# A two-layer attention and SwiGLU trunk on one core: where the bias tables are sent, and where the squares and 1/rms of the second norm stand

## The chip, the core and the metric

The kernel runs on one core of one Trainium2 chip. The metric is the device time of one execution in microseconds (us), the median of several. The engines are TensorE (PE, matmuls), VectorE (DVE), ScalarE (ACT), GpSimd (POOL) and SyncE (SP, whose queue issues nearly all DMAs). All data are float32.

## The reference, cut to what matters

Sequence and width are 1024, there are two layers. Each layer does the following, and a last RMSNorm closes the trunk.

```python
h = rms_norm(x, g_attn[l]) * (1 + sc1) + sh1          # modulated by c @ w_mod
q.., k.., v.. = split(h @ w_in[l])                    # 4 + 6 + 6 heads, three groups
# A: 2-D neighbourhood attention, bias from rpb_na[l]
# B: windowed attention, T5 bias by distance, sink logits
# C: dense attention, q/k normed, rotary
x = x + gate1 * (rms_norm_per_group(concat(A, B, C)) @ w_o[l])
h = rms_norm(x, g_ffn[l]) * (1 + sc2) + sh2
u, g = split(h @ w_gu[l]); x = x + gate2 * ((silu(u) * g) @ w_down[l])
```

## The kernel before

**Products.** Every float32 operand of a product is split into a high part and the rest (`whi`/`wlo` for weights; names that end in h and l for activations), and `mm3` (lines 205 to 208) makes three matmuls of a product. ACT makes the high part, DVE or POOL the difference (`split_tile`, 156 to 168). A weight column comes by SP into `wst`, of which there are two buffers.

**Stages.** The start turns x, makes the modulation by a matrix-vector product over `w_mod` (tiles `gm`) and does the first columns of group C. The order of PE, ACT, DVE and SP is written out there: `pin` makes an `Engine` keep the order of the text. Where no `pin` is on, a scheduler sets the order on each engine and may draw an instruction ahead of where the text has it. Then come the projections of layer 0 (A, B and C columns, then v, whose weights `wst` and `wsv` SP loads), the stream of the attention's 64 pairs, the o-projection with its residuals, gate/up, down. Layer 1 repeats this from the projections on.

**Tables.** Group A's bias comes from a skewed table in DRAM, one for each layer: three DMAs spread `rpb_na` over it, one of 930 KB and two of 248 elements by 16 by 8. Lines 828 to 837 send both tables at the end of the start. Group B's bias rows are made by `bias_rows` (1024 to 1031) in layer 0's projections: a product, a subtraction on DVE, one store to `rowB` and six broadcasts of it into `skB`, which the attention reads as `bz`. The pieces of a table overlap, so that one waits for the landing of the one before.

**The o-projection.** Its loop takes eight output columns in the order 6, 7, 0 to 5 (1847 to 1865). `residual` adds each column's product to x (tile `xb`) on DVE for the second half of the tokens. The first half is done before it: `square_sum` (400 to 411) squares its eight blocks on ACT and adds them on DVE to `ssq`; `rstd_rows` then runs in two steps, `rstd_cols` (four matmuls into `ps_st`, a root on ACT, a reciprocal on DVE) and `spread` (four transposes into `ps_r`, from which DVE reads 1/rms as a row). After the loop `square_sum` is called for the second half.

**Gate/up.** A product of 1024 by 1024 blocks is made from seven (`PRODUCTS`, 221 to 224), each of four k groups with three matmuls. For the first `EARLY = 7` column blocks q the products "11" and "21", which need the first half of the tokens alone, are made first, from the weight columns that `first_cols` loads and splits. Beside them the second half is normed: `rstd_cols` for it stands after the products of q = 0, `spread` after the first product of q = 1, and `t2_part`, `t3_part` and `t4_part` make the parts t1 to t4 and "22" of the activations (tiles `ht1h` to `ht4l`, `h22h`, `h22l`). Then the main loop makes the other products of q = 0: t2, t1, t3, "22", t4. The products "12" to "22" are combined in `gu_product`, whose copies from PSUM are `u` and `sg`; POOL multiplies `sg` by `u`, and the tile that a finished copy goes to can be one whose x block has to be read first, so that the copy ahead of "22" waits for the last part of t4.

Of the kernel before, what the change touches and what calls it, by code (L numbers as in the profile page):

```python
# [10 lines left out]
F32 = mybir.dt.float32  # L11
F32R = mybir.dt.float32r
I32 = mybir.dt.int32
AF = mybir.ActivationFunctionType
ALU = mybir.AluOpType
# [4 lines left out]
P = 128  # L20
D = 1024
S = 1024
KC = D // P
H = 512
FF = 2816
# [57 lines left out]
def bc(ap, shape):  # L83
    return ap.to_broadcast(shape)
# [3 lines left out]
def trunk(ctx: ExitStack, tc, A, C, out):  # L88
# [5 lines left out]
    def pin(engines, on):  # L94
        for e in engines:
            e.pinned = on

    def open_pool(name, bufs=1, side="left", space=None):
        kw = dict(name=name, bufs=bufs, side=side, reuse_waits="tile")
        if space is not None:  # L100
            kw["space"] = space
            if space == PSUM:
                kw.pop("side")
        cm = tc.tile_pool(**kw)
        p = cm.__enter__()
        return cm, p
# [63 lines left out]
    def split_w(src, a=1, hl=None, eng=None):  # L170


        st = stage()
        for dst, s in src(parts(st, a)):
            sp.dma_start(dst, s)
        return split_tile(st, a, hl, eng)
# [101 lines left out]
            self.fill()  # L278
            return self.have.pop(0)

    def product(num, banks, bank, a, b, m):
        if num in (1, 2, 5):
            banks[bank] = psl.tile([P, 512], F32, name="ps_w", tag="mm")
        ps = banks[bank]
        for k in range(m):
            mm3(
                ps, a[0][:, k], a[1][:, k], b[0][:, k], b[1][:, k],
                num in (1, 2, 5) and k == 0, k == m - 1, skip_group_check=True,
            )
        return ps  # L290


# [104 lines left out]
            yield  # L397


    def square_sum(ntp, xt, half, bufs=2):  # L400
        ssq = ntp.tile([P, H], F32, name="ssq", tag="ssq", bufs=bufs)
        c = slice(half * H, (half + 1) * H)
        for n in range(KC):
            if n == 0:
                act.activation(ssq, xt[:, n, c], AF.Square)
                continue
            sq = ntp.tile([P, H], F32, name="sq", tag="sq", bufs=2)
            act.activation(sq, xt[:, n, c], AF.Square)
            dve.tensor_tensor(out=ssq, in0=ssq, in1=sq, op=ALU.add)
        return ssq  # L410

    def rstd_cols(ssqs, width, nt, sp_, psp, tag="mm", newton=False):

# [330 lines left out]
    ps = spread(rxs[0], 0, psl)  # L744
# [80 lines left out]
    for n in (4, 6):  # L825
        h_blocks(1, rows, (n, n + 1))
    sp.dma_start(sinkc, bc(A["sink_sw"].rearrange("l h -> (l h)")[None, :], [P, 12]))
    for l in range(2):
        rpb = A["rpb_na"][l].rearrange("h i d -> (h i d)")
        for o, n in ((OVER, 1860), (0, OVER), (OVER + 1860, OVER)):  # L830
            sp.dma_start(
                bass.AP(
                    tensor=skA[l].tensor, offset=skA[l].offset + o,
                    ap=[[8 * LA + 31, 16], [LA + 1, 8], [1, n]],
                ),
                bc(rpb[None, None, 0:n], [16, 8, n]),
            )
    pin((pe, act, dve, sp), False)
    close(s2_cm)
    dve.tensor_scalar(out=sinkc, in0=sinkc, scalar1=-1.0, scalar2=None, op0=ALU.mult)  # L840
# [3 lines left out]
    for l in range(2):  # L844
# [14 lines left out]
        def qk_tile():  # L859
            return qkp.tile([P, 5, S], F32R, name="qk", tag="qk", bufs=2)  # L860
# [161 lines left out]
        def bias_rows():  # L1022


            ps = psl.tile([P, 512], F32, name="ps_b", tag="mm")
            for i in range(2):
                pe.matmul(ps[0:6], t5h[:, i, :], oneh, start=(i == 0), stop=(i == 1))
            dve.tensor_tensor(out=mB, in0=mB, in1=ps[0:6], op=ALU.subtract)
            sp.dma_start(rowB, mB)
            for h in range(6):  # L1030
                sp.dma_start(skB[h], bc(rowB[h][None, :], [P, 512]))

# [619 lines left out]
        for n in range(-AHEAD - 1, N + 1):  # L1654
# [19 lines left out]
                what()  # L1674
            if n == 50:
                yq = qk_tile()
            if n == 8:
                edges_make()
            if n == 54:
# [67 lines left out]
        def residual(ps, n, c, g0):  # L1747
            dve.scalar_tensor_tensor(
                out=xt[:, n, c], in0=ps, scalar=mod[:, g0 + n : g0 + n + 1], in1=xt[:, n, c],
                op0=ALU.mult, op1=ALU.add,  # L1750
            )
# [88 lines left out]
        def h_shift_split(b, i, src, sh):  # L1840
            hi, lo = (t[:, i] for t in hb[b])
            act.activation(hi, src, AF.Identity, bias=sh)
            shifted_sub(lo, src, sh, f32(hi))

        mp_cm, mp = open_pool("mp", side="left")
        ssq = square_sum(ntp, xt, 0, 1)
        for i, n in enumerate((6, 7, 0, 1, 2, 3, 4, 5)):
            w = wc[i] if i < KC - NK else w_next()
            if i < 4:
                spill(0, range(2 * i, 2 * i + 2))  # L1850
            ps = psl.tile([P, 512], F32, name="ps_o", tag="mm")
            o_cols(
                ps, w, range(8), lambda ki: y1[0][:, korder[ki], :],
                lambda ki: y1[1][:, korder[ki], :],
            )
            residual(ps, n, slice(H, S), 16)
            if i == 1:
                norm = rstd_rows(ssq, ntp, psl)
                next(norm)
            if i == 3:  # L1860
                rows = next(norm)
                for k in range(KC):
                    h_norm(k, 0, rows)
                    h_shift_split(("11", "21")[k % 2], k // 2, xt[:, k, 0:H], shift(k))
        ssq = square_sum(ntp, xt, 1, 1)
        spill(1)
        close(mp_cm)
        close(y1_cm)
# [41 lines left out]

        sg, quads = {}, {}

        def gu_product(q, p, a):
            num, b, bank = p
            up = q % 2
            t = quads.setdefault(q, {})
            ps = product(num, t, bank, a, hb[b], 4)
            e, o = sg.get(q // 2, (None, None))
            lo, hi = slice(0, H), slice(H, S)

# [74 lines left out]
            sg[b] = [x_tile(4 + 2 * (b % 2) + i, [P, S], "sg") for i in range(2)]  # L1995


        def first_cols(c0):
            rows = w_gu[:, c0 : c0 + P].rearrange("(k h p) n -> h p k n", h=2, p=P)
            return split_w(  # L2000
                lambda v: [(v[:, 4 * i : 4 * i + 4], rows[i]) for i in range(2)], KC, eng=dve
            )

        dsh = ffp.tile([P, 4], F32, name="dsh")
        for i in range(4):
            sub(dsh[:, i : i + 1], shift(2 * i + 1), shift(2 * i))
        EARLY = 7
        early = [first_cols(q % 2 * FF + q // 2 * 2 * P) for q in range(4)]
        raw0 = None
        spare = cp.tile([P, 1024], F32, name="spare", tag="acc")  # L2010

# [27 lines left out]

        mods_due = mod_stream(psl, (ntp, "sq", 2, H), (l + 1, 1 - l))  # L2040
        bs = []
        rows = None
        norm = rstd_rows(ssq, ntp, psl)
        ahead = Ahead(gu_parts())
        for q in range(EARLY):
            for i in range(2):
                a = [w[:, 4 * i : 4 * i + 4] for w in early[q]]
                gu_product(q, PRODUCTS[i], a)
                if (q, i) == (1, 0):
                    rows = next(norm)  # L2050
            if q + 4 < EARLY:
                early.append(first_cols((q + 4) % 2 * FF + (q + 4) // 2 * 2 * P))
            elif raw0 is None:
                raw0 = gu_raw(0)
            if q == 0:
                next(norm)
            if 1 <= q < 5:
                bs.append(t2_part(q - 1, rows))
            if q == 1:
                t3_part(0, *bs[0])  # L2060
                t4_part(0, *bs[0])
            if q == EARLY - 2:
                ahead.fill(5)
# [360 lines left out]
```

## Time and profile before

| | us |
|---|---|
| median of 3 runs | 2408.71 |
| range of the runs | 2406.3 to 2409.22 |
| the profiled execution | 2405.48 |
| its span | 2403.5 |
| PE busy in it | 2354.1 |
| DVE busy | 1783.6 |
| ACT busy | 1203.9 |
| POOL busy | 760.7 |

The page of the profile gives busy times by engine, the span in slices, and the costliest groups. A row of the timeline gives the start, the busy time, the engine, the line, the operation with its tiles (out <- in) and shape, how many of them stand in the row, and in square brackets how long the engine was idle before it and what ended that. All instructions of the engines carry L51, the line of the helper that issues them, so that they are told apart by their tiles. SPq is SP's queue of DMA issues. A row of the windows gives the busy time of engines in a stretch, with the clock that PE was granted (1.00 is full speed), the busy share of the DMA engines and the GB/s. A row of the waits gives what an engine waited for: us in total, times, and the longest.

### The profile page before, as it was taken

The numbers are of one execution on the slowest core, as the hardware profiler recorded it, in microseconds if no ns is written. First come the engines' busy times: TensorE is split into PE (matmuls) and PEld (weight loads), VectorE is DVE, ScalarE is ACT, GpSimd is POOL, SyncE is SP. The second block draws the span as 40 slices with busy tenths as digits, with TensorE's granted clock in tenths as the row PEclk, the third lists the DMA queues.
The fourth block names the chain that finished last, engine by engine and source line by source line (L and its number), as shares of the span: only waits on it lengthen the run. The fifth ranks groups of instructions, "written<-read, shape, count | busy, mean of one in ns | idle before, by whom it ended". The sixth has DMA issues, their size and how long they took to land. (4 is left out here: it accounts for less than half of the span.)

```text
span 2403.5 us, 34024 instructions
## 1 busy us (share of the span) xinstructions
PE 2354.1 (98%) x11953; PEld 1966.3 (82%) x11953; DVE 1783.6 (74%) x2826; ACT 1203.9 (50%) x2296; POOL 760.7 (32%) x767
## 2 busy tenths in 40 slices
PE   8999999999999999999999999999999999999998
PEld 5788898788788888888888889987878888888786
DVE  6757898977957776497866689988787675537765
ACT  5322888944543433344533158897454334334443
POOL 1522445610344444200145224464005443430001
PEclk9999999999999999999999999999999999999999
DMA  8667206064345343687434841332634443329643
GB/s 292 170 184 241 73 12 183 18 210 129 105 142 166 127 149 101 194 255 248 150 108 126 256 122 27 81 113 74 212 103 132 145 146 106 117 91 295 210 127 109
DMA packets 300497, 351.40 MB, mean 146 GB/s; under 512 B 51620, under 2 KB 221948, under 8 KB 300328
## 3 DMA queue, kind: packets, MB, share of 16 engines
q1 hardware_dynamic: 277368, 332.85, 44.2%
q10 hardware_dynamic: 21504, 12.59, 2.0%
q0 software_dynamic: 1456, 3.81, 0.4%
q8 instruction: 94, 1.54, 0.3%
q14 instruction: 75, 0.61, 0.1%
HBM read 267.38 MB, written 85.79 MB: 147 GB/s over the span
## 5 line engine op out<-in xcount | busy, mean ns | idle before, releaser
L51 PE MATMUL ps_d<-wpt 128*128 128x512 f32 x1848 | 425.8, 391 | 3.3 <-ACT wpt L51 1.5
L51 PEld LDWEIGHTS ps_d<-wpt 128*128 128x128 f32 x1848 | 345.3, 188 | 78.7 <-DVE wpt L51 2.9
L51 POOL TENSOR_SCALAR pr<-pr,rs 128x384 f32<-128x384 f32 (+2 forms) x252 | 191.9, 775 | 282.4 <-DVE rs L51 260.1
L51 POOL TENSOR_TENSOR sg<-sg,u 128x512 f32<-128x512 f32 x86 | 124.4, 1448 | 352.1 <-ACT sg L51 227.9
L51 PE MATMUL pv<-pt,vs 128*128 128x256 f32 x1088 | 180.9, 296 | 7.2 <-DVE y L51 3.3
L51 DVE TENSOR_TENSOR pt<-T,pt 128x512 fp32r<-128x512 f32 x272 | 178.1, 681 | 9.4 <-ACT pt L51 7.8
L51 ACT COPY u<-ps_w 128x512 f32<-128x512 f32 x128 | 75.2, 587 | 209.3 <-PE ps_w L51 209.3
L51 PE MATMUL T<-identr,pr 128*128 128x128 f32 x1176 | 173.3, 273 | 1.0 <-ACT rb L51 0.6
L51 ACT CAST pt<-T 128x512 fp32r<-128x512 f32 x272 | 152.7, 586 | 39.7 <-PE T L51 37.4
L51 POOL TENSOR_TENSOR wpt<-ws,wpt 128x512 fp32r<-128x512 f32 x80 | 112.4, 1406 | 179.2 <-ACT wpt L51 137.9
L51 ACT CAST wpt<-w 128x512 fp32r<-128x512 f32 x154 | 95.5, 620 | 137.2 <-PE ps_d L51 129.2
L51 PEld LDWEIGHTS pv<-pt,vs 128*128 128x128 f32 x1088 | 144.6, 189 | 22.1 <-DVE y L51 11.7
L51 DVE TENSOR_TENSOR wpt<-w,wpt 128x512 fp32r<-128x512 f32 x154 | 111.0, 720 | 64.7 <-ACT wpt L51 64.3
L51 PEld LDWEIGHTS T<-identr,pr 128*128 128x128 f32 x1176 | 138.7, 140 | 17.3 <-ACT rb L51 1.0
L51 DVE SCALAR_TENSOR_TENSOR acc<-wmt,condT,acc 128x512 f32<-128x512 f32 (+1 forms) x98 | 104.7, 1078 | 63.8 <-DMA wmt<-in_w_mod_dram 63.4
L51 ACT CAST wpt<-ws 128x512 fp32r<-128x512 f32 x176 | 107.8, 622 | 63.4 <-PE ps_w L51 26.8
L51 ACT CAST wpt<-graw 128x512 fp32r<-128x512 f32 x154 | 95.0, 617 | 72.7 <-DMA graw<-gpd 61.0
L51 DVE TENSOR_TENSOR wpt<-ws,wpt 128x512 fp32r<-128x512 f32 x96 | 87.0, 915 | 54.0 <-ACT wpt L51 53.9
L51 DVE TENSOR_REDUCE rs<-sC 128x1 f32<-128x1024 f32 x96 | 116.5, 1218 | 12.2 <-PE sC L51 10.8
L51 DVE TENSOR_TENSOR wlo<-wst,whi 128x1024 fp32r<-128x1024 f32 x68 | 85.6, 1260 | 49.5 <-ACT whi L51 45.5
L51 ACT CAST whi<-wst 128x1024 fp32r<-128x1024 f32 x70 | 73.2, 1049 | 93.0 <-PE ps_o L51 46.6
L51 DVE TENSOR_TENSOR wpt<-graw,wpt 128x512 fp32r<-128x512 f32 x154 | 110.3, 716 | 10.9 <-ACT wpt L51 10.9
(301 smaller groups left out, 6103.1 us busy)
## 6 DMA issues: line engine op xcount, KB each, us to landing
wr<-in_w_gu_dram SPq DMA_DIRECT2D x92, 512.0 KB, 4.3
gpd<-sg SPq DMA_DIRECT2D x154, 256.0 KB, 4.5
graw<-gpd SPq DMA_DIRECT2D x76, 512.0 KB, 3.7
w<-in_w_down_dram SPq DMA_DIRECT2D x110, 256.0 KB, 5.4
wmt<-in_w_mod_dram SPq DMA_DIRECT2D x48, 512.0 KB, 5.8
qk<-qkd SPq DMA_DIRECT2D x44, 512.0 KB, 7.1
wst<-in_w_o_dram SPq DMA_DIRECT2D x32, 512.0 KB, 4.2
wmt<-in_w_mod_dram SPq DMA_DIRECT2D x64, 256.0 KB, 4.5
```

What stands on the lines that cost most here:

```text
L51: ins = op(*args, **kwargs)
```

## The change

Four edits go together.

- The table of layer 1 and the six broadcasts into `skB` are issued in the text of layer 0's attention (n is the pair): `skB` at n = 1, 3 and 5, the table at n = 7. Layer 0's table stays where it was.
- `square_sum` becomes a generator that takes the blocks in the residuals' order 6, 7, 0 to 5. The second half's squares start after the residual at i = 4 and go on with one block for each residual.
- The first weight columns of gate/up are loaded within the o loop: column 0 at i = 4, FF and 2P at i = 6, FF + 2P behind it. ACT and DVE keep the written order from the residual at i = 5 until the end of q = 0.
- 1/rms stands inside the second product of q = 0: `rstd_cols` after its k = 0, `spread` after k = 2. `product` and `gu_product` take a table of calls for that.

```diff
@@ -278,7 +278,7 @@
             self.fill()
             return self.have.pop(0)
 
-    def product(num, banks, bank, a, b, m):
+    def product(num, banks, bank, a, b, m, inside=()):
         if num in (1, 2, 5):
             banks[bank] = psl.tile([P, 512], F32, name="ps_w", tag="mm")
         ps = banks[bank]
@@ -287,6 +287,8 @@
                 ps, a[0][:, k], a[1][:, k], b[0][:, k], b[1][:, k],
                 num in (1, 2, 5) and k == 0, k == m - 1, skip_group_check=True,
             )
+            if k in inside:
+                inside[k]()
         return ps
 
 
@@ -397,17 +399,17 @@
             yield
 
 
-    def square_sum(ntp, xt, half, bufs=2):
-        ssq = ntp.tile([P, H], F32, name="ssq", tag="ssq", bufs=bufs)
+    def square_sum(ntp, xt, half, order):
+        ssq = ntp.tile([P, H], F32, name="ssq", tag="ssq", bufs=1)
         c = slice(half * H, (half + 1) * H)
-        for n in range(KC):
-            if n == 0:
+        for n in order:
+            if n == order[0]:
                 act.activation(ssq, xt[:, n, c], AF.Square)
-                continue
-            sq = ntp.tile([P, H], F32, name="sq", tag="sq", bufs=2)
-            act.activation(sq, xt[:, n, c], AF.Square)
-            dve.tensor_tensor(out=ssq, in0=ssq, in1=sq, op=ALU.add)
-        return ssq
+            else:
+                sq = ntp.tile([P, H], F32, name="sq", tag="sq", bufs=2)
+                act.activation(sq, xt[:, n, c], AF.Square)
+                dve.tensor_tensor(out=ssq, in0=ssq, in1=sq, op=ALU.add)
+            yield ssq
 
     def rstd_cols(ssqs, width, nt, sp_, psp, tag="mm", newton=False):
 
@@ -825,7 +827,7 @@
     for n in (4, 6):
         h_blocks(1, rows, (n, n + 1))
     sp.dma_start(sinkc, bc(A["sink_sw"].rearrange("l h -> (l h)")[None, :], [P, 12]))
-    for l in range(2):
+    def table(l):
         rpb = A["rpb_na"][l].rearrange("h i d -> (h i d)")
         for o, n in ((OVER, 1860), (0, OVER), (OVER + 1860, OVER)):
             sp.dma_start(
@@ -835,6 +837,8 @@
                 ),
                 bc(rpb[None, None, 0:n], [16, 8, n]),
             )
+
+    table(0)
     pin((pe, act, dve, sp), False)
     close(s2_cm)
     dve.tensor_scalar(out=sinkc, in0=sinkc, scalar1=-1.0, scalar2=None, op0=ALU.mult)
@@ -1027,8 +1031,6 @@
                 pe.matmul(ps[0:6], t5h[:, i, :], oneh, start=(i == 0), stop=(i == 1))
             dve.tensor_tensor(out=mB, in0=mB, in1=ps[0:6], op=ALU.subtract)
             sp.dma_start(rowB, mB)
-            for h in range(6):
-                sp.dma_start(skB[h], bc(rowB[h][None, :], [P, 512]))
 
 
 
@@ -1674,6 +1676,11 @@
                 what()
             if n == 50:
                 yq = qk_tile()
+            if l == 0 and n in (1, 3, 5):
+                for h in (n - 1, n):
+                    sp.dma_start(skB[h], bc(rowB[h][None, :], [P, 512]))
+            if l == 0 and n == 7:
+                table(1)
             if n == 8:
                 edges_make()
             if n == 54:
@@ -1842,9 +1849,16 @@
             act.activation(hi, src, AF.Identity, bias=sh)
             shifted_sub(lo, src, sh, f32(hi))
 
+        def first_cols(c0):
+            rows = w_gu[:, c0 : c0 + P].rearrange("(k h p) n -> h p k n", h=2, p=P)
+            return split_w(
+                lambda v: [(v[:, 4 * i : 4 * i + 4], rows[i]) for i in range(2)], KC, eng=dve
+            )
+
         mp_cm, mp = open_pool("mp", side="left")
-        ssq = square_sum(ntp, xt, 0, 1)
-        for i, n in enumerate((6, 7, 0, 1, 2, 3, 4, 5)):
+        *_, ssq = square_sum(ntp, xt, 0, order)
+        order = (6, 7, 0, 1, 2, 3, 4, 5)
+        for i, n in enumerate(order):
             w = wc[i] if i < KC - NK else w_next()
             if i < 4:
                 spill(0, range(2 * i, 2 * i + 2))
@@ -1853,7 +1867,20 @@
                 ps, w, range(8), lambda ki: y1[0][:, korder[ki], :],
                 lambda ki: y1[1][:, korder[ki], :],
             )
+            if i == 5:
+                pin((act, dve), True)
             residual(ps, n, slice(H, S), 16)
+            if i == 4:
+                squares = square_sum(ntp, xt, 1, order)
+                early = [first_cols(0)]
+                for _ in range(4):
+                    next(squares)
+            if i == 6:
+                early.append(first_cols(FF))
+            if i > 3:
+                ssq = next(squares)
+            if i == 6:
+                early.append(first_cols(2 * P))
             if i == 1:
                 norm = rstd_rows(ssq, ntp, psl)
                 next(norm)
@@ -1862,7 +1889,6 @@
                 for k in range(KC):
                     h_norm(k, 0, rows)
                     h_shift_split(("11", "21")[k % 2], k // 2, xt[:, k, 0:H], shift(k))
-        ssq = square_sum(ntp, xt, 1, 1)
         spill(1)
         close(mp_cm)
         close(y1_cm)
@@ -1910,11 +1936,11 @@
 
         sg, quads = {}, {}
 
-        def gu_product(q, p, a):
+        def gu_product(q, p, a, inside=()):
             num, b, bank = p
             up = q % 2
             t = quads.setdefault(q, {})
-            ps = product(num, t, bank, a, hb[b], 4)
+            ps = product(num, t, bank, a, hb[b], 4, inside)
             e, o = sg.get(q // 2, (None, None))
             lo, hi = slice(0, H), slice(H, S)
 
@@ -1995,17 +2021,11 @@
             sg[b] = [x_tile(4 + 2 * (b % 2) + i, [P, S], "sg") for i in range(2)]
 
 
-        def first_cols(c0):
-            rows = w_gu[:, c0 : c0 + P].rearrange("(k h p) n -> h p k n", h=2, p=P)
-            return split_w(
-                lambda v: [(v[:, 4 * i : 4 * i + 4], rows[i]) for i in range(2)], KC, eng=dve
-            )
-
         dsh = ffp.tile([P, 4], F32, name="dsh")
         for i in range(4):
             sub(dsh[:, i : i + 1], shift(2 * i + 1), shift(2 * i))
         EARLY = 7
-        early = [first_cols(q % 2 * FF + q // 2 * 2 * P) for q in range(4)]
+        early.append(first_cols(FF + 2 * P))
         raw0 = None
         spare = cp.tile([P, 1024], F32, name="spare", tag="acc")
 
@@ -2039,21 +2059,21 @@
 
         mods_due = mod_stream(psl, (ntp, "sq", 2, H), (l + 1, 1 - l))
         bs = []
-        rows = None
         norm = rstd_rows(ssq, ntp, psl)
         ahead = Ahead(gu_parts())
+        found = []
+        inside = {0: lambda: next(norm), 2: lambda: found.append(next(norm))}
         for q in range(EARLY):
             for i in range(2):
                 a = [w[:, 4 * i : 4 * i + 4] for w in early[q]]
-                gu_product(q, PRODUCTS[i], a)
-                if (q, i) == (1, 0):
-                    rows = next(norm)
+                gu_product(q, PRODUCTS[i], a, inside if (q, i) == (0, 1) else ())
+            if q == 0:
+                pin((act, dve), False)
+                rows = found[0]
             if q + 4 < EARLY:
                 early.append(first_cols((q + 4) % 2 * FF + (q + 4) // 2 * 2 * P))
             elif raw0 is None:
                 raw0 = gu_raw(0)
-            if q == 0:
-                next(norm)
             if 1 <= q < 5:
                 bs.append(t2_part(q - 1, rows))
             if q == 1:
```

What the scheduler makes of it is read from the order of the instructions. On SP near the beginning of the start (`skA_91` is layer 0's table, `skA_92` layer 1's; a plus is a row that only the changed kernel has):

```order
 L51 DMA gm<-in_w_mod_dram 128x4x256 x2
 L51 DMA wst<-in_w_in_dram 128x2x512
+L51 DMA skA_92<-in_rpb_na_dram 16x8x1860
 L51 DMA gm<-in_w_mod_dram 128x4x256 x4
 L51 DMA wst<-in_w_in_dram 128x2x512
```

The large piece of layer 1's table has moved from the projections to the start, ahead of four gm loads. On SP between the projections and the v weights of layer 0 (the last row is the first v weight):

```order
 L51 DMA qkd<-qko 512x1x64 x2
 L51 DMA skA_91<-in_rpb_na_dram 16x8x248
-L51 DMA skA_92<-in_rpb_na_dram 16x8x1860
 L51 DMA qkd<-qko 512x1x64
 L51 DMA rowB<-mB 6x512
-L51 DMA skA_92<-in_rpb_na_dram 16x8x248
-L51 DMA skB<-rowB 128x512 x3
-L51 DMA skA_92<-in_rpb_na_dram 16x8x248
-L51 DMA skB<-rowB 128x512 x3
 L51 DMA qkd<-qko 512x1x64 x4
 L51 DMA wst<-in_w_in_dram 128x2x256
```

Nothing of layer 1's table and of skB stands ahead of the v weights any more; the six broadcasts and the last small piece now stand among the wmt loads behind the v weights. On DVE of the kernel before, around 1/rms of layer 0's gate/up:

```order
L51 TENSOR_TENSOR dsh<-vecs_85 128x1 x4
L51 TENSOR_TENSOR wlo<-wst,whi 128x1024
L51 TENSOR_TENSOR ssq<-ssq,sq 128x512 x3
L51 TENSOR_TENSOR u<-u,ps_w 128x512
L51 TENSOR_TENSOR wlo<-wst,whi 128x1024
L51 RECIPROCAL rstd<-rstd 128x4
L51 SCALAR_TENSOR_TENSOR xb<-xb,vecs_85,ps_r 128x512 x2
L51 TENSOR_TENSOR xb<-xb 128x512
```

The same place in the changed kernel:

```order
L51 TENSOR_TENSOR ssq<-ssq,sq 128x512
L51 TENSOR_TENSOR dsh<-vecs_85 128x1 x4
L51 TENSOR_TENSOR wlo<-wst,whi 128x1024
L51 RECIPROCAL rstd<-rstd 128x4
L51 SCALAR_TENSOR_TENSOR xb<-xb,vecs_85,ps_r 128x512
L51 TENSOR_TENSOR u<-u,ps_w 128x512
L51 SCALAR_TENSOR_TENSOR xb<-xb,vecs_85,ps_r 128x512
L51 TENSOR_TENSOR wlo<-wst,whi 128x1024
L51 TENSOR_TENSOR xb<-xb 128x512
```

Two of the three last additions to ssq now stand further ahead, among the residuals, and one wlo and one addition to u stand behind the first reading of 1/rms (`ps_r`) instead of ahead of it.

## The prediction

> **What bounds the kernel now.** I read the page first, then the timeline of TensorE for its idle time and its granted clock, and at each hole the engines that it waits for. The page says where a gain can lie at all:
>
> ```profile
> span 2403.5 us, 34024 instructions
> PE 2354.1 (98%) x11953; PEld 1966.3 (82%) x11953; DVE 1783.6 (74%) x2826; ACT 1203.9 (50%) x2296; POOL 760.7 (32%) x767
> ```
>
> TensorE is idle for 2403.5 - 2354.1 = 49.4 us. Anything that ACT, DVE, POOL or the queue does beside it is free unless it ends one of these few waits or lets the clock fall. The change touches three places: the v weights of layer 0, the start, and gate/up of both layers.
>
> The timeline of the v weights (SP's queue, then ACT, then PE; the square bracket is idle time before a row and what ended it), the queue's waits there, and one stretch of PE (us, PE busy, clock, DMA share, GB/s):
>
> ```profile
> 93.74 0.29 SPq L51 DMA_DIRECT2D rowB<-mB  x1
> 98.97 0.57 SPq L51 DMA_DIRECT2D skA<-in_rpb_na_dram  x1
> 106.84 4.63 SPq L51 DMA_DIRECT2D qkd<-qko  x4
> 111.51 4.01 SPq L51 DMA_DIRECT2D wst<-in_w_in_dram  x6
> SPq L51 <- DMA skA<-in_rpb_na_dram: 9.6, 3, 4.8
> 117.15 1.04 ACT L51 CAST whi<-wst 128x1024 fp32r<-128x1024 f32 x1 [7.20 <-DMA wst<-in_w_in_dram]
> 118.25 0.80 PE L51 MATMUL ps_v<-hh,whi 128*128 128x512 f32 x1 [3.83 <-ACT whi L51]
> 124.07 0.39 PE L51 MATMUL ps_v<-hl,whi 128*128 128x512 f32 x1
> 120.00:121.00 1.00, 1.00 (x4) 0.50 1.11 353
> ```
>
> SP is idle between 94.0 and 99.0 because a piece of layer 1's table waits for the piece before it to land; skB follows, and the v weights go out only at 111.5. ACT then waits 7.20 us for them and PE 3.83 us for ACT. After that wait the clock is at 0.50 in the stretch shown.
>
> The normal pace of PE, and the two places in gate/up where it waits: the last matmul of t3, the first of "22", the last of "22" and t4 together (layer 0, then layer 1), and the clock in layer 1:
>
> ```profile
> 578.53 0.39 PE L51 MATMUL ps_w<-h21h,whi 128*128 128x512 f32 x1
> 581.25 0.95 PE L51 MATMUL ps_st<-onesr,ssq 128*128 128x1 f32 x8
> 623.25 0.39 PE L51 MATMUL ps_w<-ht3l,wpt 128*128 128x512 f32 x1
> 626.92 0.72 PE L51 MATMUL ps_w<-h22h,wpt 128*128 128x512 f32 x2 [1.59 <-ACT sg L51]
> 631.83 0.39 PE L51 MATMUL ps_w<-ht2h,wpt 128*128 128x512 f32 x1
> 1792.45 0.39 PE L51 MATMUL ps_w<-ht3l,wpt 128*128 128x512 f32 x1
> 1802.61 0.39 PE L51 MATMUL ps_w<-ht2h,wpt 128*128 128x512 f32 x1
> 1797.00:1798.00 1.00, 1.00 (x4) 0.50 1.09 377
> ```
>
> Twelve matmuls take 581.25 - 578.53 = 2.72 us, 0.227 each. After t3's last start in layer 0 stand 24 matmuls of "22" and t4: 0.23 + 24 x 0.227 = 5.67 would do, 631.83 - 623.25 = 8.58 are spent: 2.91 lost. In layer 1 it is 10.16 - 5.67 = 4.49 lost, and there the clock falls to 0.50. These three holes (the v weights and gate/up twice) are what the change can gain.
>
> **The change part by part.**
>
> *The v weights.* What the queue did between 93.74 and 106.84 for layer 1's table and skB is gone from this place. The four qkd stores follow rowB at about 94.3; by their own row they take 4.63, so the first v weight goes out at 94.3 + 4.6 = 98.9 instead of 111.5, and by the row's 117.15 - 111.51 = 5.64 from issue to the split it is there at 104.5. ACT is free from 117.15 - 7.20 = 109.95, splits it by 111.0, and PE comes at 118.25 - 3.83 = 114.42. So the wait of 3.83 goes. With it goes what follows: from 118.25 to 124.07 stand eleven starts, worth 11 x 0.227 = 2.50 at the normal pace, and 5.82 were spent: 3.32. Sum: **-7.15**. Late next is ACT's splitting, 3.4 us ahead of PE, so nothing is left of the hole. Bounds: 3.83 if the clock falls anyway, 7.7 if a later wait of half a microsecond goes as well.
>
> *Layer 1's table at the start.* The text puts it into the attention, the order puts its large piece of 930 KB ahead of four gm loads near the beginning. The rows there (the queue, DVE, PE, two DMA groups, one stretch with all engines: PE, PEld, DVE, ACT, POOL, clock, DMA share, GB/s):
>
> ```profile
> 15.95 3.52 SPq L51 DMA_DIRECT2D gm<-in_w_mod_dram  x4
> 24.40 1.54 DVE L51 SCALAR_TENSOR_TENSOR ga<-gm,condT,ga 128x512 f32<-128x512 f32 x2 [0.23 <-DMA gm<-in_w_mod_dram]
> 25.08 1.88 PE L51 MATMUL ps_mod<-gm,condT 128*1 128x512 f32 x4
> 37.51 1.02 PE L51 MATMUL ps_mod<-ga,onesr 128*1 128x512 f32 x2 [1.25 <-DVE ga L51]
> skA<-in_rpb_na_dram SPq DMA_DIRECT2D x2, 930.0 KB, 6.2
> gm<-in_w_mod_dram SPq DMA_DIRECT2D x16, 512.0 KB, 8.9
> 20.00:22.00 2.00, 1.96 (x5) 0.44 (x5) 1.85 (x3) 1.19 (x2) 0.00 (x0) 1.00 1.07 353
> ```
>
> The transfers are saturated (1.07 busy at 353 GB/s), and gm needs 8.9 us to land. 930 KB at 353 GB/s are 2.7 us, so gm lands at about 27.1 instead of 24.4. PE's matmul on it, at 25.08, had 25.08 - 24.40 = 0.7 to spare, DVE 0.23; between them I take 0.9 off, since DVE's work can be made up in part, and count **+1.8**. The order of the engines is written out here, and PE still waits for DVE's ga at 37.51, so it isn't made up later. Bounds: 0, if later gaps of the queue take it; 6.2 - 0.9 = 5.3, if gm waits for the table's whole landing.
>
> *skB and the small pieces of the table.* They now go out among the wmt loads of the v projections. The queue's waits from 128 to 175 us, and two stretches there:
>
> ```profile
> SPq L51 <- DVE acc L51: 14.7, 6, 8.4
> 146.00:152.00 6.00, 6.00 (x49) 5.84 (x48) 0.00 (x0) 0.59 (x1) 0.91 (x3) 1.00 0.59 180
> 164.00:170.00 6.00, 6.00 (x52) 6.00 (x52) 0.34 (x1) 1.42 (x2) 0.00 (x0) 1.00 0.01 3
> ```
>
> SP waits 14.7 us there, PE is busy all the time and the DMA engines stand at 0.59 and 0.01. I take **0**. If the cover were gone, 1.6 MB at 353 GB/s would cost 4.5.
>
> *Gate/up.* DVE and ACT around 1/rms, the two-input operations of DVE beside POOL's multiplies, and the copy that opens "22":
>
> ```profile
> 577.33 1.23 DVE L51 TENSOR_TENSOR wlo<-wst,whi 128x1024 fp32r<-128x1024 f32 x1 [0.30 <-ACT whi L51]
> 581.52 0.69 DVE L51 TENSOR_TENSOR u<-u,ps_w 128x512 f32<-128x512 f32 x1 [0.77 <-PE ps_w L51]
> 582.30 1.23 DVE L51 TENSOR_TENSOR wlo<-wst,whi 128x1024 fp32r<-128x1024 f32 x1
> 585.56 1.40 DVE L51 SCALAR_TENSOR_TENSOR xb<-xb,vecs,ps_r 128x512 f32<-128x512 f32 x2 [1.95 <-PE ps_r L51]
> 618.93 1.28 DVE L51 TENSOR_TENSOR ht3l<-xb,ht3h 128x512 fp32r<-128x512 f32 x2
> 622.79 3.47 DVE L51 TENSOR_TENSOR ht4l<-xb,ht4h 128x512 fp32r<-128x512 f32 x2
> 622.31 3.39 POOL L51 TENSOR_TENSOR sg<-sg,u 128x512 f32<-128x512 f32 x2 [112.72 <-ACT sg L51]
> 626.29 0.58 ACT L51 COPY sg<-ps_w 128x512 f32<-128x512 f32 x1 [1.97 <-DVE ht4l L51]
> ```
>
> Before, the sums and ps_r stand behind the second and the third product, and the norm starts at 585.56. Now ps_st is behind the third matmul of the second product (578.53 + 3 x 0.23 = 579.2) and ps_r behind the ninth (about 581.0), so the norm starts at about 582.2: 3.4 earlier. But one wlo (1.23) and one u (0.69) that stood ahead of it now stand behind, so DVE gives h's last parts only 3.4 - 1.9 = 1.5 earlier. The order also has no t4 group ahead of "22" any more, 3 x 0.227 = 0.7 of cover. Per layer 1.5 - 0.7 = 0.8 is left. In layer 1 the clock was at 0.50 in the hole; the other 4.49 - 2.91 = 1.6 lie there, and with a shorter wait I take them as gone. Sum: 0.8 + 0.8 + 1.6 = **-3.2**. Bounds: if POOL's multiplies no longer meet ht4l (3.47 for two where ht3l took 1.28: 2.2 of stall), 2.2 more per layer, but no more than the hole holds: -6.5 in all; if both fall ahead of it, below nothing: the wait is then 0.4 longer than before in layer 0 and the rest of layer 1's is as it was: +0.5. That the squares come earlier costs PE nothing itself: the matmuls are the same.
>
> One rule bears on layer 1's 1.6. The Trainium skill, page "TensorE: Matmul & The Clock Gate", section "Part 1: The HAM clock gate (the "warmup" mystery)", says that the clock halves after an idle window of about 3.4 us; by it no wait under that would cost clock, and the gain would be the 3.2 that I count. The trace agrees at 118.25 (3.83 of wait, then 0.50) and does not in layer 1, where the clock fell after shorter waits. The sum with the clock still falling there would be 1.6 less.
>
> *Sum:* -7.15 + 1.8 + 0 - 3.2 = -8.55. The profiled run took 2405.48 us, 1.98 beyond its span, and would take 2396.9; the median of the runs shown, 2408.71, lies 3.2 above, and the forecast is for such a median: 2400.2 us. About 0.2%, 4.8 us, is what a measurement of this kernel can tell from no change.
>
> **The rivals.**
>
> *POOL holds DVE longer.* ht4l's second part follows ACT's work that also releases POOL's second multiply, so both multiplies may lie ahead of it. Then gate/up gives -0.5 instead of 3.2. For it: the two rows at 622 overlap, and 3.47 against 1.28 is a stall. Against: DVE comes 1.5 earlier and may be through. Time 2400.2 + 3.7 = 2403.9. The Trainium skill, page "SBUF — State Buffer", section "Who interferes with whom", has a DVE instruction with two inputs in SBUF contend with a GpSimd one that reads SBUF; by that rule, the trace agrees.
>
> *The start loses a whole landing.* 5.3 instead of 1.8: 2403.7. For it: the queue is saturated. Against: 6.2 includes the time in which the other transfers run on beside it.
>
> *The hole at the v weights stays*, because something else holds the queue or ACT, and the change does not do there what it removes: only 1.4 of net gain is left, 2407.3. Against: ACT had been idle 7.20, and SP's long wait is on the table itself.
>
> *Slower: a late weight column ties 1/rms.* ACT and DVE are now held in the written order, in which the split of the fourth early column stands ahead of the reciprocal. These columns arrive just in time:
>
> ```profile
> 576.24 1.05 ACT L51 CAST whi<-wst 128x1024 fp32r<-128x1024 f32 x1 [2.10 <-DMA wst<-in_w_gu_dram]
> wst<-in_w_o_dram SPq DMA_DIRECT2D x32, 512.0 KB, 4.2
> ```
>
> The split ended at 577.33 + 1.23 = 578.6, and PE wants 1/rms at 581.0: 2.2 to spare with the reciprocal. If the column lands s late, PE stands for s - 2.2 inside the second product with everything behind it, and 3.3 of clock may follow as at 118.25. One landing and a half of 4.2, s = 6, gives 7.1 per layer: 2408.7 - 5.4 + 14.2 = 2417.5. It decides from 2 x (s + 1.1) = 5.4 + 4.8, so from s = 4. Against: the order moves no load behind another store here.
>
> **How the numbers follow.** The forecast has 0.60. POOL's stall has 0.16 and the start's landing 0.09; their times lie at the edge of 0.2% (2403.9), so I give 0.15 of the 0.25 to faster and 0.10 to no change. The hole that stays has 0.08, no change. The late column has 0.07, slower. That makes 0.75 faster, 0.18 the same, 0.07 slower. Low end: 7.7 gained at the v weights, 0 lost at the start, 6.5 in gate/up: 2394.5. High end: both middle rivals lie below 2404 alone, together at 2407.4; I stop at 2405.5, which leaves out the hole that stays, the late column and their coincidence.
>
> **What would show it.** In the profile after: the v weights' first issue near 99 us and no wait of PE near 118; gm landing near 27 and the start's end later by 1 to 3 us; the first norm of gate/up about 3.4 earlier against the second product; the hole between t3 and "22" 0.8 shorter in layer 0 and the clock at 1.00 in layer 1. Wrong would be: PE waiting for ps_st or ps_r's operands inside the second product, a ht4l pair of over 3 us with "22" as late as before, or a v projection that still waits for ACT.

## The result and the profile after

The changed kernel takes 2399.48 us, the median of five (2397.76 to 2402.58), against 2408.71 before (five executions by now, 2406.3 to 2411.36). The ratio is 0.9964, with an interval of 0.9954 to 0.9975: 6.0 to 11.1 us faster. The forecast was 2400.2; the same kernel timed once more below has 2401.84, so that a hit to 0.7 us is closer than the measurement itself. The profiled execution took 2402.58 and is the slowest of the five; what it lost against the others is shown below.

First the busy times on the page of the changed kernel, whose span is 2400.5 us:

```profile
PE 2353.8 (98%) x11953; PEld 1966.7 (82%) x11953; DVE 1784.9 (74%) x2826; ACT 1204.3 (50%) x2296; POOL 759.8 (32%) x767
```

PE has the same matmuls and the same busy time; what changed is when it waits and at what clock it runs.

**The v weights.** The timeline of SP and PE of the changed kernel, with the clock in the stretch that stood at 0.50 before:

```profile
95.65 0.29 SPq L51 DMA_DIRECT2D rowB<-mB  x1
96.05 2.57 SPq L51 DMA_DIRECT2D qkd<-qko  x4
98.67 3.37 SPq L51 DMA_DIRECT2D wst<-in_w_in_dram  x6
116.20 0.46 PE L51 MATMUL ps_v<-hh,whi 128*128 128x512 f32 x1
118.81 0.39 PE L51 MATMUL ps_v<-hl,whi 128*128 128x512 f32 x1
120.00:121.00 1.00, 1.00 (x6) 1.00 1.02 193
```

The first v weight goes out at 98.67 (forecast 98.9, before 111.51). That it meets the forecast is luck in part: rowB is issued 1.9 later than before, because the start has become longer, and the four qkd stores take 2.57 instead of the 4.63 that the forecast took over from the row before. No row of ps_v has a bracket any more: PE comes to a split that is there. The eleven starts from 116.20 to 118.57 take 118.81 - 116.20 = 2.61 us instead of 5.82, at full clock.

**The start.** The same rows of DVE and PE as before, and the queue:

```profile
13.67 0.69 SPq L51 DMA_DIRECT2D skA<-in_rpb_na_dram  x1
16.28 5.50 SPq L51 DMA_DIRECT2D gm<-in_w_mod_dram  x4
26.84 1.54 DVE L51 SCALAR_TENSOR_TENSOR ga<-gm,condT,ga 128x512 f32<-128x512 f32 x2 [2.35 <-DMA gm<-in_w_mod_dram]
26.86 1.88 PE L51 MATMUL ps_mod<-gm,condT 128*1 128x512 f32 x4 [1.37 <-DMA gm<-in_w_mod_dram]
39.29 1.02 PE L51 MATMUL ps_mod<-ga,onesr 128*1 128x512 f32 x2 [1.25 <-DVE ga L51]
```

gm lands at 26.84 instead of 24.40. PE's product on it stands at 26.86 instead of 25.08, 1.78 later. Some twelve us on, the product on DVE's ga stands at 39.29 instead of 37.51, still 1.78 later.

**Gate/up.** In the changed kernel, PE's transposes of 1/rms and DVE's first reading of them in layer 0; PE around t3 and "22" with the last matmul of t1 ahead of them and the first one behind; and the same ends in layer 1:

```profile
578.22 0.60 PE L51 MATMUL ps_r<-identr,rstd 128*128 128x128 f32 x4
578.86 0.75 DVE L51 SCALAR_TENSOR_TENSOR xb<-xb,vecs,ps_r 128x512 f32<-128x512 f32 x1 [1.48 <-PE ps_r L51]
617.24 0.39 PE L51 MATMUL ps_w<-ht1l,wpt 128*128 128x512 f32 x1
618.50 0.73 PE L51 MATMUL ps_w<-ht3h,wpt 128*128 128x512 f32 x2 [0.87 <-ACT sg L51]
622.27 0.73 PE L51 MATMUL ps_w<-h22h,wpt 128*128 128x512 f32 x2 [0.76 <-ACT sg L51]
627.85 0.65 PE L51 MATMUL ps_w<-ht2h,wpt 128*128 128x512 f32 x2
1788.67 0.39 PE L51 MATMUL ps_w<-ht1l,wpt 128*128 128x512 f32 x1
1789.94 0.73 PE L51 MATMUL ps_w<-ht3h,wpt 128*128 128x512 f32 x2 [0.87 <-ACT sg L51]
1799.30 0.62 PE L51 MATMUL ps_w<-ht2h,wpt 128*128 128x512 f32 x2
1797.00:1798.00 1.00, 1.00 (x6) 1.00 0.00 0
```

The kernel before has the last matmul of t1 at:

```profile
620.53 0.39 PE L51 MATMUL ps_w<-ht1l,wpt 128*128 128x512 f32 x1
1789.73 0.39 PE L51 MATMUL ps_w<-ht1l,wpt 128*128 128x512 f32 x1
```

The norm starts 578.86 - 572.52 = 6.34 us behind the first matmul of gate/up, before 585.56 - 575.81 = 9.75: 3.4 earlier, as forecast. From the last matmul of t1 to the first one behind t4 stand 37 starts, 8.40 us at the normal pace. Before, 631.83 - 620.53 = 11.30 were spent in layer 0 and 1802.61 - 1789.73 = 12.88 in layer 1: 2.90 and 4.48 lost. After, 627.85 - 617.24 = 10.61 and 1799.30 - 1788.67 = 10.63: 2.21 and 2.23 lost. So gate/up gained 0.69 and 2.25, of which 1.6 is clock. But the hole has another shape: before it lay between t3 and "22"; now half of it lies ahead of t3, where nothing waited before.

### The profile page after: what moved, and what is told of

Its sections match the earlier page's. It is cut to its first block, busy times and chain, and to the rows that moved or that the text cites. A ratio compares the mean times of both kernels' runs of the same rounds, so it can differ in the third digit from the quotient of the medians.

```text
span 2400.5 us, 34016 instructions
## 1 busy us (share of the span) xinstructions
PE 2353.8 (98%) x11953; PEld 1966.7 (82%) x11953; DVE 1784.9 (74%) x2826; ACT 1204.3 (50%) x2296; POOL 759.8 (32%) x767
## 5 line engine op out<-in xcount | busy, mean ns | idle before, releaser
L51 DVE TENSOR_TENSOR ws<-wr 128x512 f32<-128x512 f32 x88 | 84.3, 960 | 47.9 <-POOL wpt L51 44.1
L51 DVE TENSOR_TENSOR wpt<-graw,wpt 128x512 fp32r<-128x512 f32 x154 | 110.6, 718 | 12.6 <-ACT wpt L51 12.5
```

What stands on the lines that cost most here:

```text
L51: ins = op(*args, **kwargs)
```

## The experiments

Medians and ratios are against the kernel before on the same chip; the kernels of one group stand beside each other.

**1. Tables alone** (`tables_only`). The kernel before, with

```diff
-    for l in range(2):
+    def table(l):
...
+    table(0)
...
-            for h in range(6):
-                sp.dma_start(skB[h], bc(rowB[h][None, :], [P, 512]))
...
+            if l == 0 and n in (1, 3, 5):
+                for h in (n - 1, n):
+                    sp.dma_start(skB[h], bc(rowB[h][None, :], [P, 512]))
+            if l == 0 and n == 7:
+                table(1)
```

> Of the change only the tables and the bias rows are moved; squares, early columns and 1/rms stand as in the kernel before. Theory (the hole at the v weights was the queue's, the start pays for the 930 KB ahead of gm, gate/up is a separate gain): 7.0 gained at the v weights, 1.8 lost at the start, 5.2 us faster than before, about 2403.5, and gate/up as before, with PE's waits of 0.73 and 1.59 between t3 and 22. Rival (the hole and gate/up share something, such as the phase in which the loads arrive): gate/up's hole changes by over 1 us in this kernel as well.

Measured: 2405.47, ratio 0.9981 (0.9972 to 0.9989), 2.6 to 6.7 us faster. PE has no wait at the v weights, and in gate/up "22" waits as in the kernel before:

```profile
624.69 0.74 PE L51 MATMUL ps_w<-h22h,wpt 128*128 128x512 f32 x2 [1.58 <-ACT sg L51]
```

The two parts of the change are separate, as the theory had it; 5.2 lies in the interval. What no run separates is the table from the six broadcasts of skB: both were taken out of SP's way together.

**2. Norm alone** (`norm_only`). The changed kernel with both tables and skB sent as in the kernel before, the edit above the other way round.

> Of the change only the squares, the early columns, the pinned stretch and the place of 1/rms; the tables and bias rows are sent as in the kernel before. Theory: 0.8 to 1.0 gained in gate/up of layer 0 and 2.2 to 2.4 in layer 1, 3.2 us faster than before, about 2405.5; at the v weights PE's wait of 3.8 with the clock at 0.50 behind it stays; gm lands as before. Rival (the whole gain is at the v weights, and gate/up's shorter waits are lost again behind it): no difference to before that can be measured.

Measured: 2406.9, ratio 0.9987 (0.9978 to 0.9996), 1.0 to 5.3 us faster. The wait at the v weights is there, and gate/up has the changed kernel's two waits:

```profile
118.05 0.80 PE L51 MATMUL ps_v<-hh,whi 128*128 128x512 f32 x1 [3.10 <-ACT whi L51]
624.64 0.73 PE L51 MATMUL ps_w<-ht3h,wpt 128*128 128x512 f32 x2 [0.88 <-ACT sg L51]
628.41 0.74 PE L51 MATMUL ps_w<-h22h,wpt 128*128 128x512 f32 x2 [0.74 <-ACT sg L51]
```

The rival (no difference) lies outside the interval, if only just. The two parts make (1 - 0.9981) + (1 - 0.9987) = 0.0032 of 2408.7, 7.7 us; the whole change makes 8.7.

**3. A later table** (`late_table`). The changed kernel, with layer 1's table ordered on SP behind the DMA that the text has before it:

```diff
             if l == 0 and n == 7:
+                sp.last = sp.any
+                pin([sp], True)
                 table(1)
+                pin([sp], False)
```

(`sp.any` is the last DMA of SP, noted by `Engine`.)

> The changed kernel, with layer 1's table held behind the broadcasts of the bias rows, so that its 930 KB go out among the wmt loads of the v projections and not at the start. Theory (the start's loss is the 2.7 us that gm's landing is put off by this transfer): gm lands as in the kernel before, the start loses nothing, and the kernel is 1.8 us faster than the changed one, about 2397.7. Rival 1 (the start's loss is something else, or is made up): the same time as the changed kernel. Rival 2 (the wmt loads have no room for 930 KB more): PE waits after the v projections, and the kernel is 1 to 3 us slower than the changed one.

Measured: 2399.97, ratio 0.9954 (0.9941 to 0.9966). The queue has the large piece at 146, among the wmt loads; DVE's and PE's rows of gm:

```profile
23.73 2.40 DVE L51 SCALAR_TENSOR_TENSOR ga<-gm,condT,ga 128x512 f32<-128x512 f32 x3
25.41 1.88 PE L51 MATMUL ps_mod<-gm,condT 128*1 128x512 f32 x4
114.67 0.46 PE L51 MATMUL ps_v<-hh,whi 128*128 128x512 f32 x1
```

Neither has a wait, and PE comes to the v weights at 114.67 instead of 116.20: 1.53 of the start's 1.78 were the table's, the rest stood already ahead of it. Rival 2 falls: PE waits nowhere behind the v projections for it. PE is still 1.3 ahead when the attention begins (first `sC` at 221.00 against 222.34). The gain over the changed kernel is seen in the trace alone: the medians, 2399.97 and 2399.48, show none, and the intervals overlap widely.

**4. POOL's multiplies on DVE** (`mult_dve`). The changed kernel with

```diff
-                    pool.tensor_tensor(out=e, in0=e, in1=quads[q]["11"], op=ALU.mult)
+                    dve.tensor_tensor(out=e, in0=e, in1=quads[q]["11"], op=ALU.mult)
```

> The changed kernel, with POOL's multiplies of the early blocks' sg by u made on DVE, where they fall behind the second part of t4. Theory (POOL's two multiplies hold DVE by 1.04 us each while DVE makes the parts that the copies ahead of t3 and 22 wait for): PE's waits ahead of t3 (1.0) and 22 (0.9) go in both layers, 3 to 4 us faster than the changed kernel, about 2396. Rival (what holds PE there is the chain of the x blocks itself, the stall is beside it): the waits stay and the time is that of the changed kernel within 1 us.

The changed kernel has these rows of DVE and POOL ahead of the two waits; the first of DVE's opens t3, the second "22":

```profile
615.53 1.78 DVE L51 SCALAR_TENSOR_TENSOR xb<-xb,vecs,t 128x512 f32<-128x512 f32 x1
619.16 1.78 DVE L51 SCALAR_TENSOR_TENSOR h22l<-xb,vecs,h22h 128x512 fp32r<-128x512 f32 x1
615.23 1.54 POOL L51 TENSOR_TENSOR sg<-sg,u 128x512 f32<-128x512 f32 x1 [108.91 <-ACT sg L51]
619.06 1.33 POOL L51 TENSOR_TENSOR sg<-sg,u 128x512 f32<-128x512 f32 x1 [2.29 <-ACT sg L51]
```

The experiment has the same DVE operations, PE's t3 and "22", and layer 1 behind t4:

```profile
614.95 0.75 DVE L51 SCALAR_TENSOR_TENSOR xb<-xb,vecs,t 128x512 f32<-128x512 f32 x1
617.54 0.75 DVE L51 SCALAR_TENSOR_TENSOR h22l<-xb,vecs,h22h 128x512 fp32r<-128x512 f32 x1
616.90 0.73 PE L51 MATMUL ps_w<-ht3h,wpt 128*128 128x512 f32 x2
619.75 0.63 PE L51 MATMUL ps_w<-h22h,wpt 128*128 128x512 f32 x2
1795.22 0.50 PE L51 MATMUL ps_w<-ht2h,wpt 128*128 128x512 f32 x1 [0.51 <-DVE wpt L51]
```

An operation of 0.75 takes 1.78 when POOL's multiply runs beside it; without that both of PE's waits are gone, 1.9 us in each layer. Some of it is given back just behind, where DVE's wpt is now late (0.51). Measured: 2398.3, ratio 0.9948 (0.9935 to 0.996), 9.6 to 15.7 us faster than before. Theory and trace agree. By the centres it is 3.8 us ahead of the changed kernel (12.5 against 8.7), as expected, but the two intervals overlap by 1.5, and by the trace 1.3 of the 1.9 are kept to the end of the early column blocks in each layer, 2.6 in all (table below).

**5. The changed kernel and the kernel before once more** (`after_b`, `before_b`), without an edit.

> The changed kernel once more, beside the next ones. Theory (the profiled execution of the changed kernel lost 1.6 us at 437 us and some 2 us near 1122 us by falls of the clock that have nothing to do with the change): median about 2399.5, and a profile with such losses at other places or none. Rival (the change brings them): the same two falls at the same places, and not in a second profile of the kernel before.

> The kernel before once more, one profile. Theory: the waits at the v weights (3.8) and in gate/up (0.73 and 1.59 in both layers) are there again, and a fall of the clock at 437 us as in all five later profiles, since the attention is the same; its first profile was the odd one, and stood 3.2 us below its median for that. Rival: no fall at 437 us, as in the first profile, so that the change's parts bring it.

Measured: the changed kernel 2401.84, ratio 0.997 (0.9957 to 0.9982). The windows of PE (us, busy, clock, DMA share, GB/s) of the first profile of the changed kernel, then of the second:

```profile
433.00:436.00 3.00, 3.00 (x17) 0.61 0.00 0
1121.00:1124.00 3.00, 3.00 (x9) 0.56 0.12 43
432.00:433.00 1.00, 1.00 (x6) 0.50 0.00 0
```

```profile
433.00:436.00 3.00, 3.00 (x25) 1.00 0.00 0
1121.00:1124.00 3.00, 3.00 (x15) 1.00 0.35 52
```

The 0.61 and 0.56 are means of windows that are partly at full clock; the clock itself stands at 0.50, as the narrower window shows. The same kernel has the falls in one execution and not in the other, so they are no fixed cost of the change. Whether the change makes them more frequent isn't settled: of the twelve profiles, nine are of kernels with some part of the change, and five of these have the fall near 433; the three of kernels without have none. The theory of `before_b` was wrong in its own part: the kernel before has no fall at 437 in its second profile either. Its wait at the v weights is another size there, and in layer 1's gate/up the clock stays at 1.00:

```profile
117.08 0.80 PE L51 MATMUL ps_v<-hh,whi 128*128 128x512 f32 x1 [2.24 <-ACT whi L51]
626.49 0.73 PE L51 MATMUL ps_w<-h22h,wpt 128*128 128x512 f32 x2 [1.60 <-ACT sg L51]
1793.00:1797.00 4.00, 2.70 (x11) 1.00 0.05 8
1797.00:1801.00 4.00, 2.97 (x13) 1.00 1.00 324
```

So of what the first profile of before lost, some of the wait at the v weights and the 1.6 of clock in layer 1 are not lost in every execution.

**6. 1/rms at its old place** (`old_rms`). The changed kernel, with

```diff
-                gu_product(q, PRODUCTS[i], a, inside if (q, i) == (0, 1) else ())
+                gu_product(q, PRODUCTS[i], a)
+                if (q, i) == (1, 0):
+                    rows = next(norm)
...
+            if q == 0:
+                next(norm)
```

> The changed kernel, with the sums and the spreading of 1/rms back behind the first and the second product as in the kernel before; squares, early columns and pinned stretch stay. Theory (gate/up's gain comes from the norm that starts about 3 us earlier, because 1/rms stands inside the second product): the norm starts some 3 us later again, t4's first group stands ahead of 22 again, the holes are 2.9 in layer 0 and 4 to 4.5 in layer 1 with the clock at 0.50, and 3 us of the changed kernel's time are given back, about 2402.5. Rival (the earlier squares and columns bring the gain, the place of 1/rms does not matter): as the changed kernel within 1 us.

Measured: 2404.63, ratio 0.9981 (0.9972 to 0.9989), 2.8 us behind the changed kernel beside it (2401.84). The norm and the waits:

```profile
580.37 1.41 DVE L51 SCALAR_TENSOR_TENSOR xb<-xb,vecs,ps_r 128x512 f32<-128x512 f32 x2 [1.95 <-PE ps_r L51]
619.18 0.73 PE L51 MATMUL ps_w<-ht4h,wpt 128*128 128x512 f32 x2 [0.73 <-ACT u L51]
621.73 0.73 PE L51 MATMUL ps_w<-h22h,wpt 128*128 128x512 f32 x2 [1.59 <-ACT sg L51]
1791.87 1.22 PE L51 MATMUL ps_w<-h22h,wpt 128*128 128x512 f32 x2 [1.59 <-ACT sg L51]
```

The intervals of the two kernels overlap, so the trace has to decide. The norm again starts 580.37 - 570.62 = 9.75 behind the first matmul, and with the squares early and 1/rms late gate/up is that of the kernel before, 1.22 for two matmuls in layer 1 telling of the low clock. The rival falls: the place of 1/rms carries the gain. That the early squares are needed for that place was not tested.

**7. Without the pinned stretch** (`no_pin`). The changed kernel without `pin((act, dve), True)` at i = 5 and its end.

> The changed kernel without the pinned stretch of ACT and DVE; squares, early columns and 1/rms stay where the change has them in the text, and the scheduler puts one split of a weight column further ahead on both engines. Theory (the gain comes from the place of 1/rms on PE, and the fourth column's split stands ahead of the reciprocal in either order): norm and holes as in the changed kernel, the same time within 1 us. Rival (the pinned order is what keeps DVE free for the reciprocal): PE waits ahead of the transposes inside the second product, and 1 to 3 us are lost.

Measured: 2401.98, ratio 0.9969 (0.9957 to 0.9981), as the changed kernel (0.997). No wait comes up ahead of the transposes. The pinned order does nothing for the time that these runs can tell.

**8. POOL's multiplies on DVE in the kernel before** (`before_mult`): the edit of 4 in the kernel before.

> The kernel before with one edit: the early multiplies of sg by u on DVE instead of POOL, where they fall behind the second part of t4. Theory (half of the hole in gate/up before was POOL holding DVE, 2.2 of the 3.47 us of the two ht4l): the ht4l pair takes about 1.3, 22 starts about 2 earlier in each layer, of which some 0.6 are given back in the next products as in the other kernel with this edit; 2 to 4 us faster than before. Rival (in the kernel before the late 1/rms holds 22 whatever POOL does, and only the change makes POOL count): the hole stays at 2.9, no difference to before.

```profile
622.41 1.29 DVE L51 TENSOR_TENSOR ht4l<-xb,ht4h 128x512 fp32r<-128x512 f32 x2
624.79 0.62 PE L51 MATMUL ps_w<-h22h,wpt 128*128 128x512 f32 x2
630.39 0.51 PE L51 MATMUL ps_w<-ht2h,wpt 128*128 128x512 f32 x1 [0.65 <-ACT wpt L51]
```

The pair takes 1.29 instead of 3.47, "22" starts without a wait, 0.65 is given back behind it. The hole closes as the theory had it, but in the time it does not show: 2408.07, ratio 0.9993 (0.9985 to 1.0002), between 3.6 faster and 0.5 slower. The 2 to 4 us that were expected lie at the end of the interval. The trace says why it is less: "22" starts 1.75 earlier, but half of that is given back in the next products, and 0.9 a layer is left at the end of the early column blocks (table below).

**9. Both edits on the changed kernel** (`late_mult`): those of 3 and 4.

> The changed kernel with both other edits: layer 1's table held among the wmt loads, and the early multiplies of sg by u on DVE. Theory (the two gains lie at different places of PE's path and add up): 1.5 at the start and 3.0 in gate/up, 4.5 us faster than the changed kernel, about 2395. Rival (one is lost again in a later wait that both run into): no faster than the better of the two alone, about 2398.

Measured: 2396.52, ratio 0.9951 (0.9939 to 0.9963), beside 2401.84 of the changed kernel: 5.3 less, where 4.5 was expected. It is the fastest median of the study. The ratio's interval overlaps those of 3 and 4 alone, so that the sum is shown against the changed kernel's median and not against each single edit. By the trace, 1.5 at the start and 1.3 in each layer's gate/up make 4.1.

## Why the prediction was right, point by point

*The v weights, -7.15.* The first profile pair shows it: PE went from 3.83 of wait and 5.82 for eleven starts to none and 2.6, 7.0 in all. The 3.32 that the forecast put down to the clock holds a wait of 0.47 for DVE's wlo as well. The term was read from one execution of before. From the first `ps_ab` to the first transpose behind the v weights (`ps_t`), the four profiles with the old tables (before, before_b, before_mult, norm_only) take 64.85, 63.99, 63.80 and 65.57, and the changed kernel 58.28 and 58.26: 5.5 to 7.3 gained. Experiment 1 shows that the tables and skB alone bring it (58.32).

*The start, +1.8.* gm was forecast for 27.1 and landed at 26.84; PE was 1.78 later, 1.53 of it the table's by experiment 3. The parts came out as well: the landing moved by 2.44 (2.7 forecast), and PE had 0.68 of that to spare. The rival in which gm waits for a whole landing (5.3) fell.

*skB among the wmt loads, 0.* No wait of PE behind the v projections came up.

*Gate/up, -3.2.* Measured 0.69 and 2.25 in the hole, 2.9. Over the whole stretch from the first matmul of t2 (`ht2h`) to the first "11" product behind the early column blocks (`h11h` with `wpt`), in us:

| kernel | layer 0 | layer 1 |
|---|---|---|
| before | 98.38 | 99.68 |
| before_b (clock at 1.00) | 98.38 | 98.38 |
| old_rms | 98.40 | 99.69 |
| the changed kernel | 97.48 | 97.47 |
| after_b | 97.49 | 97.50 |
| mult_dve | 96.17 | 96.18 |
| before_mult | 97.50 | 97.51 |

So the hole is worth 0.9 in each layer, and the clock 1.3 in layer 1 where it falls. The earlier norm is the cause (experiment 6). The size was right for a partly wrong reason. The step "DVE gives h's last parts only 1.5 earlier, 0.7 of cover goes" took the parts to move together. In fact t3 now waits as well, because POOL's first multiply also starts earlier against PE and falls on DVE's xb ahead of the copy that t3 needs, and the second falls on h22l ahead of the second ht4l. That is the condition of the first rival, "both multiplies may lie ahead of it": it came true, and its price of +0.5 was wrong. Each multiply costs DVE 1.03 (1.78 against 0.75), 2.06 for two, but the kernel before lost 2.18 to them already (3.47 against 1.29 for the ht4l pair, experiment 8). So the stall did not grow, and "22" starts 1.37 earlier against t2 (10.24 us behind it instead of 11.61), close to the 1.5 that was forecast. Experiment 4 puts the two stalls at 1.9 us a layer for PE, of which 1.3 are kept. The stall itself is what the Trainium skill, page "SBUF — State Buffer", section "Who interferes with whom", lets one expect: both DVE operations have two inputs in SBUF, and POOL reads SBUF beside them. The trace agrees, with 1.78 against 0.75.

*The clock in layer 1, 1.6 of the 3.2.* It is gone in both profiles of the changed kernel, and in norm_only, late_table and no_pin. Of the four profiles with the old hole, three have the fall (before, tables_only, old_rms), and the second profile of before has the clock at 1.00 there with the same waits. So this part is a loss of some executions, and no fixed cost. The rule that was weighed against it (the Trainium skill, page "TensorE: Matmul & The Clock Gate", section "Part 1: The HAM clock gate (the "warmup" mystery)") would have no fall at waits this short; the runs show falls after 0.73 and 1.59, and at 433 us one with PE busy throughout. Here the measurements decide. Nor does the fall at the v weights bear the rule out as the prediction had it: the clock is low before the wait of 3.83 is over, and in the second profile of before it is low behind a wait of 2.24.

```profile
117.00:118.00 1.00, 0.00 (x0) 0.51 0.90 253
119.00:120.00 1.00, 1.00 (x4) 0.50 1.11 353
```

The first row is the first profile of before, where PE waits from 114.42 to 118.25, the second row the second profile.

*The slower rival, a late weight column.* It did not come. The spare was smaller than the 2.2 that the text gave it. The rows of DVE in the changed kernel:

```profile
575.48 1.23 DVE L51 TENSOR_TENSOR wlo<-wst,whi 128x1024 fp32r<-128x1024 f32 x1 [0.27 <-ACT whi L51]
577.20 0.18 DVE L51 RECIPROCAL rstd<-rstd 128x4 f32<-128x4 f32 x1 [0.50 <-ACT rstd L51]
```

The split ends at 576.71, the reciprocal at 577.38, and PE's transposes start at 578.22: 0.5 until the reciprocal waits for the column, and 1.3 until PE does. A later column than that was not tried.

*The sum.* -8.55 was forecast, and the ratio gives 6.0 to 11.1. The parts as the traces have them, 5.5 to 7.3 at the v weights, 1.8 lost at the start, 0.9 in gate/up of each layer and up to 1.3 of clock, make 5.5 to 8.6. The two first profiles differ by only 2.9 (2405.48 and 2402.58), because the changed one's clock fell at 433 and 1122 us; whoever had only that pair would have read a third of the gain.

## What to carry to other kernels

Look what a queue does ahead of loads that an idle engine waits for: here moving a table and six broadcasts out of SP's way took away a wait of 1.6 to 3.8 us (four profiles) and the low clock behind it, and putting one piece of it into a saturated start cost 1.5. Where instructions are not held in order, the text's place is not the place: the table written into the attention went to the start, and only a dependency kept it where it was harmless. When a chain is moved earlier, ask which operations of another engine move with it and now run beside it: two POOL multiplies of 1.3 to 1.5 us, which PE does not wait for, held it up by 1.9 us through DVE, and 1.3 of that was lost for good.

## What the runs showed of the hardware

The clock granted to PE falls to 0.50 for some 3 us at places that differ between executions of the same program, at 433 us with PE busy throughout the stretch, and at 1122 us in the same profile, there behind a wait of 1.9. Two profiles of one kernel differ by 1 to 2 us (spans 2403.5 and 2404.9 before, 2400.5 and 2398.4 after). In the changed kernel such falls can account for it; in the kernel before it is the profile with fewer falls that is the longer, so they are not the whole of it. A DVE operation with two inputs in SBUF of 0.75 us takes 1.78 when a POOL multiply of 1.3 to 1.5 us runs beside it.
